# The projection's bank first in attention's PSUM pool, and the last tile's half columns one after the other at the end of a two-layer diffusion backbone

## The chip, the cores and the metric

The kernel runs on one core of a Trainium2 chip. The core has five engines with a queue each: TensorE (PE) for matrix products, VectorE (DVE) and ScalarE (ACT) for elementwise work, GpSimd (POOL), and SyncE (SP), which issues most transfers between the chip's memory (HBM) and the core's SBUF. TensorE writes its products to PSUM, eight banks of 128 rows by 512 float32 values; DVE and ACT read them there. The metric is the device time of one launch in microseconds (us), the median of several runs.

## The reference, cut to what matters

512 latent tokens and 256 context tokens of width 1024 pass through two layers. Layer 0 mixes tokens by windowed attention with 16 query heads and 4 key heads, layer 1 by a gated MLP over chunks of 128 tokens. Each is followed by a dense SwiGLU feed-forward network with hidden width 2816. Both halves of a layer are wrapped in RMS norms and modulated by a conditioning vector:

```python
x = x + g_ml * rmsnorm(y_l, norm_g[i, 1])
f_l = swiglu(modulate(rmsnorm(x, norm_g[i, 2]), sh_fl, sc_fl), ffn_w_in[i], ffn_w_out[i])
x = x + g_fl * rmsnorm(f_l, norm_g[i, 3])
```

The last line, in layer 1, is the end of the program: for each token, the second product of the feed-forward network is divided by the root of its own mean square over all 1024 columns, multiplied by a row of gains, added to `x` and stored.

## The kernel before

Products are made at float32 precision from two rounded parts of each operand ("high", a cast on ACT, and "low", a subtraction on DVE), three matmuls for one: high by high, high by low, low by high. Tokens are handled in four tiles of 128, numbered 0 to 3.

**The order is written out by hand.** Every piece of work is a small function. `at(time, step, ...)` files it in a plan under a name made of the function and its arguments, such as `q_step_2_0` or `c3square_y_0_512`. A long string, `ORDER`, lists all names, and `run_plan` calls the steps in the order of that list. Scheduling is manual: each engine executes its instructions in the order in which the steps issued them, and waits in its queue where an operand or a buffer isn't ready. Times given to `at` matter only for names that the list lacks.

**PSUM pools.** The first stage (norms, transposes, keys, values and the first query projections) uses the pool `psA` with all eight banks, one tile per bank. Its last tiles are two query projections (`q0`, read by `q_rows_0` and `q_rows_1`, L952) and six transposed key tiles (`kT`, `k_turn`, L1030), each read by a cast on ACT into `khi` (L414) and a subtraction on DVE into `klo` (L421). Then `psA` is closed, and attention opens two pools in the same banks: `psL`, with two double-bank tiles for scores (`s_ps`, banks 0-1 and 2-3), and `psR`, on the right side, with four single banks for three tags: `q` (one bank, the projections of later query heads, `q_ps`), `pT` (two banks, transposed probabilities) and `o` (one bank, the product with the values, `o_ps`). A tag gets its banks when it is first asked for, the first tag the lowest, bank 4. One line asks for a tile of `o` ahead of everything, so before the change `o` has bank 4, `q` bank 5, and `pT` banks 6 and 7. A new tile waits for the last reader of the tile of the older pool in its bank, and for no other. In the program as it is laid out, the last tenant of `psA` is `q0` of `q_rows_1` in bank 4, the `kT` of `k_turn_0_0` in bank 5, and the `kT` of `k_turn_2_0` in bank 1.

**Attention.** After the key transposes, TensorE's queue holds `q_step_2_0` to `q_step_2_7` (L872): 24 matmuls that project the third pair of query heads into one `q_ps` tile, from weight unit 3 (`whigh_3_*`, `wlow_3_*`). Behind them stand the first scores `score_0_0` and `score_0_1` (L1110). Then, for 16 blocks of 128 queries by 4 heads: `bound` on DVE (L1116), `exp` on ACT (L1121), `normalise` on POOL (L1137), transposes on TensorE (`turn`, L1143) copied by ACT and DVE (`turned`, L1150), the product with the values into `o_ps` (`value`, L1159), and its copy to SBUF on ACT (`store`, L1165). `store_15` is the last of them. The output projection follows in the pool `psM`, whose tiles take banks 0, 7, 6, 5, 4, 3, 2, 1 in this order: `work_0_0` (L481) writes `y00` to bank 0 and `y01` to bank 7, in turn.

**The end of the program.** In layer 1, the last two units of the feed-forward network's second weight matrix (86 and 87) are multiplied plainly: `plain7_9_t` and `plain7_10_t` (L1868) add their part for token tile `t` to two banks, `y[t][0]` for columns 0 to 511 and `y[t][1]` for 512 to 1023. A whole step is 12 matmuls that alternate between the two banks; tile 3 is done by half columns, `plain7_9_3_(0,)` and so on, 6 matmuls each. Earlier parts of the same sums are added by DVE (`add7_*`, L1858) and must be in the banks before. The operands of units 86 and 87 are `whigh`, `wlow` and `take7_18` to `take7_21`.

For each tile, a chain ends the layer: `square_y` on ACT (L441) gives the sum of squares of each half, `gain_y` on DVE (L1341) multiplies by the gains, then the reciprocal root, then `add_x` on DVE (L1345), then `store` (a transfer that SP issues, L411). ACT and DVE take turns on a bank. For tiles 0, 1 and 2 the root is made by `rstd_y`: a small instruction on DVE (L450) and a power on POOL (L451). For tile 3 it is made on ACT: `bias_y` (DVE, L1328), `root_y` (ACT, L1332), `invert_y` (DVE, L1335), and `add_x` and `store` are issued for each half.

The order of TensorE's steps there, before the change: 9_2, 9_3 columns 1, 9_3 columns 0, 9_0, 10_3 columns 0, 10_3 columns 1, 10_2, 10_0, 9_1, 10_1. So tile 3 is finished early and tile 1 last.

Of the kernel before, what the change touches and what calls it, by code (L numbers as in the profile page):

```python
# [7 lines left out]
F32 = mybir.dt.float32  # L8
# [6 lines left out]
P = 128  # L15
# [372 lines left out]
f1a7_high_4_0 f1a7_low_4_0 f1product7_4_0 f1w7_high_4_2 f1add7_p7_1 f1add7_p7d_1 f1add7_p7d_0 f1w7_low_4_2 f1add7_c12_0  # L388
f1add7_c22_0 f1take7_18 f1a7_high_4_3 f1a7_low_4_3 f1t7_add_3_21 f1take7_19 f1product7_4_1 f1w7_high_4_3 f1product7_4_2
f1w7_low_4_3 f1product7_4_3 whigh_86_1 whigh_87_0 wlow_86_1 f1add7_c21_0 f1add7_c11_0 f1add7_c22_1 whigh_87_1  # L390
f1plain7_9_2 wlow_87_1 f1add7_c21_1 f1plain7_9_3_(1,) wlow_87_0 f1plain7_9_3_(0,) f1plain7_9_0 f1take7_20 f1take7_21
f1plain7_10_3_(0,) c3square_y_0_512 f1plain7_10_3_(1,) c3square_y_512_1024 c3gain_y_0_512 c3bias_y c3root_y
c3gain_y_512_1024 c3invert_y f1plain7_10_2 c3add_x_512_1024 c3store_512_1024 c2gain_y_0_512 c2gain_y_512_1024
f1add7_c12_1 c2square_y_0_512 c2square_y_512_1024 c2rstd_y#4 f1plain7_10_0 c0square_y_512_1024 c0square_y_0_512
c2add_x#4 c0gain_y_0_512 c0gain_y_512_1024 f1plain7_9_1 c0rstd_y#4 c0add_x#4 c0store f1plain7_10_1 c3add_x_0_512
c1square_y_0_512 c1gain_y_0_512 c3store_0_512 c1square_y_512_1024 c1rstd_y#4 c1gain_y_512_1024 c2store c1add_x#4 c1store
""".split()


# [1 line left out]
def backbone_kernel(ctx: ExitStack, tc: tile.TileContext, a, out):  # L401
# [58 lines left out]
    def big(name):  # L460
        return base.tile([P, 2 * D], F32, name=name, tag="big", bufs=2)
# [403 lines left out]
    q_ps = {}  # L865
# [206 lines left out]
    psL_p = psL.__enter__()  # L1072
    psR = pool("psR", space=PSUM, side="right")
    psR_p = psR.__enter__()
    psR_p.tile([P, 512], F32, name="o_ps", tag="o", bufs=1)
    oT = [big("oT0"), big("oT1")]

    def bank_t(name):
# [1180 lines left out]
```

## Time and profile before

| what | us |
|---|---|
| median of three runs | 1101.46 |
| the three runs | 1101.46, 1100.64, 1102.72 |
| the profiled execution, device time | 1101.11 |
| its span, first to last instruction | 1099.3 |

The profile comes from one execution. Its span is 1.81 us shorter than that execution's device time, which itself is 0.35 us below the median. Rows of the timeline have the start in us from the span's start, the duration in us, the engine, the source line, the operation, the tiles written and read, the shapes, how many alike follow each other, and in brackets the engine's idle time before and what ended it. "PEld" is TensorE loading its stationary operand, "SPq" a transfer being issued, not its duration.

### The profile page before, as it was taken

The page shows a single profiled execution, that of the slowest core. Times are in us where ns is not written, and L with a number is a line of the kernel's source. Part 1 is how long each engine was busy: PE and PEld are TensorE (multiplying, and loading weights), DVE is VectorE, ACT ScalarE, POOL GpSimd, SP SyncE. Part 2 cuts the span into 40 slices and gives each one's busy share as a digit, 9 for nine tenths or more (in the row PEclk, how much of TensorE's full clock was granted, in tenths as well). Part 3 has the DMA queues.
Part 4 walks back from the last instruction along what each step waited for, and adds up shares of the span by engine and source line. Part 5 has one row for each costly group of instructions (what it writes and reads, how often), then busy time and mean ns, then how long its engine had stood idle before and what let it go on. Part 6 is the DMA issues. An engine that isn't in the chain of part 4 may idle for free.

```text
span 1099.3 us, 17847 instructions
## 1 busy us (share of the span) xinstructions
PE 1078.4 (98%) x6894; PEld 950.6 (86%) x6894; DVE 941.6 (86%) x1383; ACT 601.9 (55%) x1058; POOL 264.7 (24%) x267
## 2 busy tenths in 40 slices
PE   8979999999999999999999999999999999999997
PEld 5767777778899999998888888888999999998885
DVE  5896998938999999998988878968988798977985
ACT  6455777646654555456655534346544544556562
POOL 1624777435700000002321402007400000003300
PEclk9999999999999999999999999999999999999999
DMA  9764341346225465569964478543243334378831
GB/s 364 259 196 128 107 154 48 115 154 211 87 81 179 154 194 171 197 220 277 229 132 153 137 237 299 179 165 96 77 152 118 135 115 166 94 258 194 209 76 77
DMA packets 50393, 181.26 MB, mean 165 GB/s; under 512 B 5370, under 2 KB 9722, under 8 KB 39172
## 3 DMA queue, kind: packets, MB, share of 16 engines
q1 hardware_dynamic: 42756, 165.44, 43.6%
q0 software_dynamic: 7552, 14.68, 8.0%
q8 instruction: 54, 0.88, 0.3%
q14 instruction: 31, 0.25, 0.1%
HBM read 171.71 MB, written 2.10 MB: 158 GB/s over the span
## 4 chain that ended last, share of the span: by engine, by line
PE 90%; DVE 4%; DMA 1%; POOL 1%; issue 1%; ACT 1%; SPq 0%; DVEq 0%; ACTq 0%; POOLq 0%
PE f L1657 37%; PE y L1841 14%; PE y L481 7%; PE y L1868 6%; PE v L481 4%; PE o_ps L1159 3%; PE s_ps L1110 3%; PE pT_ps L1143 2%; PE q_ps L872 2%; PE fa L475 1%; PE fa L473 1%; PE fa L474 1%; PE u L2079 1%; PE u L2078 1%; PE u L2077 1%; POOL w_lo L421 1%
## 5 line engine op out<-in xcount | busy, mean ns | idle before, releaser
L1657 PE MATMUL f<-H,w_hi 128*128 128x256 f32 x960 | 176.3, 283 | 0.0
L1657 PEld LDWEIGHTS f<-H,w_hi 128*128 128x128 f32 x960 | 149.8, 192 | 0.3
L1657 PE MATMUL f<-H,w_lo 128*128 128x256 f32 x480 | 135.8, 283 | 0.0
L414 ACT CAST w_hi<-w_raw 128x1024 fp32r<-128x1024 f32 x90 | 93.8, 1053 | 50.6 <-PE y L481 15.6
L1841 PE MATMUL y<-w_hi,s 128*128 128x512 f32 x448 | 120.2, 389 | 0.0
L1657 PE MATMUL f<-S,w_hi 128*128 128x256 f32 x640 | 117.5, 283 | 0.0
L421 DVE TENSOR_TENSOR w_lo<-w_raw,w_hi 128x1024 fp32r<-128x1024 f32 (+1 forms) x81 | 96.9, 1200 | 22.6 <-ACT w_hi L414 22.4
L414 ACT CAST w_hi<-T 128x1024 fp32r<-128x1024 f32 x80 | 83.8, 1051 | 54.4 <-PE f L1657 33.4
L421 DVE TENSOR_TENSOR w_lo<-T,w_hi 128x1024 fp32r<-128x1024 f32 x80 | 97.0, 1219 | 11.0 <-ACT w_hi L414 10.6
L1657 PEld LDWEIGHTS f<-S,w_hi 128*128 128x128 f32 x640 | 99.9, 192 | 0.2
L1841 PEld LDWEIGHTS y<-w_hi,s 128*128 128x128 f32 x448 | 84.0, 188 | 17.7 <-ACT r L1849 0.3
L1657 PEld LDWEIGHTS f<-H,w_lo 128*128 128x128 f32 x480 | 92.1, 192 | 0.0
L1657 PE MATMUL f<-S,w_lo 128*128 128x256 f32 x320 | 90.5, 283 | 0.0
L595 POOL DMA_DIRECT2D acc<-acc x8 | 6.9, 866 | 345.4 <-DVE acc L581 339.0
L1664 ACT COPY fc<-f 128x256 f32<-128x256 f32 x120 | 43.1, 373 | 77.0 <-PE f L1657 69.6
L1829 POOL DMA_DIRECT2D t<-in_w x48 | 42.7, 975 | 165.5 <-DMA t<-in_w 87.8
L581 DVE SCALAR_TENSOR_TENSOR acc<-ada_k,sc,acc 128x1024 f32<-128x1024 f32 x56 | 71.6, 1279 | 3.6 <-DMA ada_k<-in_ada 3.3
L1841 PE MATMUL y<-w_lo,s 128*128 128x512 f32 x224 | 69.1, 390 | 0.0
L1657 PE MATMUL f<-H,x 128*128 128x256 f32 x480 | 64.4, 283 | 0.0
L1137 POOL TENSOR_SCALAR p<-p,st 128x512 f32<-128x512 f32 (+1 forms) x64 | 56.0, 907 | 34.0 <-DVE st L1133 26.1
L1116 DVE CUSTOM_DVE_ANT_0 s_ps<-s_ps,mask,nsink 128x512 f32<-128x512 f32 (+1 forms) x64 | 51.3, 820 | 14.8 <-PE s_ps L1110 13.7
L1657 PEld LDWEIGHTS f<-S,w_lo 128*128 128x128 f32 x320 | 61.4, 192 | 0.0
(265 smaller groups left out, 2760.5 us busy)
## 6 DMA issues: line engine op xcount, KB each, us to landing
w_raw<-in_w SPq DMA_DIRECT2D x67, 1024.0 KB, 5.2
ada_k<-in_ada SPq DMA_DIRECT2D x56, 512.0 KB, 4.9
ada_raw<-in_ada SPq DMA_DIRECT2D x12, 1024.0 KB, 6.2
w<-in_w SPq DMA_DIRECT2D x12, 1024.0 KB, 8.2
t<-in_w POOLq DMA_DIRECT2D x48, 256.0 KB, 6.4
ada<-in_ada SPq DMA_DIRECT2D x8, 1024.0 KB, 7.2
t<-in_w SPq DMA_DIRECT2D x8, 1024.0 KB, 8.4
w_raw<-in_w SPq DMA_DIRECT2D x10, 512.0 KB, 9.7
```

What stands on the lines that cost most here:

```text
L414: nc.scalar.copy(out=hi, in_=src)
L421: (eng or nc.vector).tensor_tensor(out=v(lo), in0=v(src), in1=v(hi).bitcast(F32), op=ALU.subtract)
L481: nc.tensor.matmul(dst, l, w[:, n * 512:(n + 1) * 512], start=first and i == 0, stop=last and i == 2)
L581: nc.vector.scalar_tensor_tensor(out=self.acc, in0=self.raws.pop(k), scalar=sc[:, k:k + 1], in1=self.acc, op0=ALU.mult, op1=ALU.add)
L1110: nc.tensor.matmul(dst, q, keys, start=i == 0, stop=i == 1)
L1116: nc.vector.tensor_tensor_reduce(out=s, in0=s, in1=self.msk, scale=-1.0, scalar=nsink[:, h:h + 1], op0=ALU.add, op1=ALU.min, accum_out=sel ...
L1137: nc.gpsimd.tensor_scalar(out=p, in0=p, scalar1=self.st[:, 12 + j:13 + j], scalar2=1.0, op0=ALU.mult, op1=ALU.mult)
L1657: nc.tensor.matmul(dst, l[:, w], r[:, k, :], start=first and k == 0 and j == 0, stop=k == 3 and j == 2, skip_group_check=True)
L1664: nc.scalar.copy(out=self.c[n][:, i * 256:(i + 1) * 256], in_=self.ps[n, 1 if i == 1 else 0])
L1829: nc.gpsimd.dma_start(out=self.tt[:, p * D + 512 * i:p * D + 512 * (i + 1)], in_=a["w"][F2[self.layer] + 1 + 2 * p + i][:, c:c + 512], acc ...
L1841: nc.tensor.matmul(self.bank7(i, j), st[:, c:c + P], w[:, z * 512:(z + 1) * 512], start=i == 1 and p == 0 and l == 0 and z == 0, stop=p == ...
L1868: nc.tensor.matmul(self.y[t][n], st[:, x + t * P:x + (t + 1) * P], parts[h][w][:, n * 512:(n + 1) * 512], start=v == 0 and h == 0 and i == ...
```

## The change

Two edits. The line that asks for a tile of `psR` ahead of everything asks for tag `q` in place of `o`. And the end of `ORDER`, from `plain7_9_2` on, is rewritten.

```diff
@@ ORDER, its last lines @@
-f1plain7_9_2 wlow_87_1 f1add7_c21_1 f1plain7_9_3_(1,) wlow_87_0 f1plain7_9_3_(0,) f1plain7_9_0 f1take7_20 f1take7_21
-f1plain7_10_3_(0,) c3square_y_0_512 f1plain7_10_3_(1,) c3square_y_512_1024 c3gain_y_0_512 c3bias_y c3root_y
-c3gain_y_512_1024 c3invert_y f1plain7_10_2 c3add_x_512_1024 c3store_512_1024 c2gain_y_0_512 c2gain_y_512_1024
-f1add7_c12_1 c2square_y_0_512 c2square_y_512_1024 c2rstd_y#4 f1plain7_10_0 c0square_y_512_1024 c0square_y_0_512
-c2add_x#4 c0gain_y_0_512 c0gain_y_512_1024 f1plain7_9_1 c0rstd_y#4 c0add_x#4 c0store f1plain7_10_1 c3add_x_0_512
-c1square_y_0_512 c1gain_y_0_512 c3store_0_512 c1square_y_512_1024 c1rstd_y#4 c1gain_y_512_1024 c2store c1add_x#4 c1store
+f1plain7_9_2 f1take7_21 f1plain7_9_0 f1add7_c21_1 f1plain7_9_3_(0,) wlow_87_0 f1take7_20 wlow_87_1 f1plain7_10_0
+c0square_y_512_1024 c0square_y_0_512 f1plain7_10_2 c2square_y_0_512 f1plain7_10_3_(0,) c0gain_y_0_512 c0rstd_y#4
+c0gain_y_512_1024 c2square_y_512_1024 f1add7_c12_1 c2gain_y_0_512 c2rstd_y#4 c0add_x#4 c0store c2gain_y_512_1024
+f1plain7_9_1 c3gain_y_0_512 c3square_y_0_512 c3bias_y c2add_x#4 f1plain7_10_1 c1square_y_0_512 c1square_y_512_1024
+c2store c1gain_y_0_512 c1rstd_y#4 c1gain_y_512_1024 c1add_x#4 c1store f1plain7_9_3_(1,) f1plain7_10_3_(1,)
+c3square_y_512_1024 c3root_y c3gain_y_512_1024 c3invert_y c3add_x_0_512 c3store_0_512 c3add_x_512_1024 c3store_512_1024
@@ attention's PSUM pools @@
     psR = pool("psR", space=PSUM, side="right")
     psR_p = psR.__enter__()
-    psR_p.tile([P, 512], F32, name="o_ps", tag="o", bufs=1)
+    psR_p.tile([P, 512], F32, name="q_ps", tag="q", bufs=1)
     oT = [big("oT0"), big("oT1")]
```

After it `q` has bank 4, `pT` banks 5 and 6 (its first tile, of `turn_0_2`, comes before the first of `o`), and `o` bank 7. The order of TensorE's last steps becomes 9_2, 9_0, 9_3 columns 0, 10_0, 10_2, 10_3 columns 0, 9_1, 10_1, 9_3 columns 1, 10_3 columns 1. Tile 0's chain comes first, then tile 2's, tile 1's, and tile 3's second half last; of tile 3's first half, the gains, the squares and the bias are done ahead of tile 1's chain. No instruction is added or removed, and the arithmetic is the same.

More of the change, by code (lines that the diff above doesn't have):

```diff
@@ L390 @@
 f1w7_low_4_3 f1product7_4_3 whigh_86_1 whigh_87_0 wlow_86_1 f1add7_c21_0 f1add7_c11_0 f1add7_c22_1 whigh_87_1
-f1plain7_9_2 wlow_87_1 f1add7_c21_1 f1plain7_9_3_(1,) wlow_87_0 f1plain7_9_3_(0,) f1plain7_9_0 f1take7_20 f1take7_21
-f1plain7_10_3_(0,) c3square_y_0_512 f1plain7_10_3_(1,) c3square_y_512_1024 c3gain_y_0_512 c3bias_y c3root_y
-c3gain_y_512_1024 c3invert_y f1plain7_10_2 c3add_x_512_1024 c3store_512_1024 c2gain_y_0_512 c2gain_y_512_1024
-f1add7_c12_1 c2square_y_0_512 c2square_y_512_1024 c2rstd_y#4 f1plain7_10_0 c0square_y_512_1024 c0square_y_0_512
-c2add_x#4 c0gain_y_0_512 c0gain_y_512_1024 f1plain7_9_1 c0rstd_y#4 c0add_x#4 c0store f1plain7_10_1 c3add_x_0_512
-c1square_y_0_512 c1gain_y_0_512 c3store_0_512 c1square_y_512_1024 c1rstd_y#4 c1gain_y_512_1024 c2store c1add_x#4 c1store
+f1plain7_9_2 f1take7_21 f1plain7_9_0 f1add7_c21_1 f1plain7_9_3_(0,) wlow_87_0 f1take7_20 wlow_87_1 f1plain7_10_0
+c0square_y_512_1024 c0square_y_0_512 f1plain7_10_2 c2square_y_0_512 f1plain7_10_3_(0,) c0gain_y_0_512 c0rstd_y#4
+c0gain_y_512_1024 c2square_y_512_1024 f1add7_c12_1 c2gain_y_0_512 c2rstd_y#4 c0add_x#4 c0store c2gain_y_512_1024
+f1plain7_9_1 c3gain_y_0_512 c3square_y_0_512 c3bias_y c2add_x#4 f1plain7_10_1 c1square_y_0_512 c1square_y_512_1024
+c2store c1gain_y_0_512 c1rstd_y#4 c1gain_y_512_1024 c1add_x#4 c1store f1plain7_9_3_(1,) f1plain7_10_3_(1,)
+c3square_y_512_1024 c3root_y c3gain_y_512_1024 c3invert_y c3add_x_0_512 c3store_0_512 c3add_x_512_1024 c3store_512_1024
 """.split()
```

## The prediction

> **What bounds the kernel now.** I read the page's busy shares first, then what TensorE waited for, then the two places that the change touches, by timeline and by windows.
>
> ```profile
> span 1099.3 us, 17847 instructions
> PE 1078.4 (98%) x6894; PEld 950.6 (86%) x6894; DVE 941.6 (86%) x1383; ACT 601.9 (55%) x1058; POOL 264.7 (24%) x267
> PE q_ps L872 <- DVE klo L421: 7.5, 1, 7.5
> PE s_ps L1110 <- ACT p L1121: 2.0, 3, 1.0
> ```
>
> TensorE is busy for 98% of the span, so time is won only where it idles or after its last matmul. Its waits, the last two lines, show one large one: 7.5 us, once, before a `q_ps` matmul, for a `klo` subtraction. A projection needs no `klo`: it reads `HA` and weights. What it waits for is its bank, which the key tile of `k_turn_0_0` still holds. The timeline of that place:
>
> ```profile
> 73.32 2.78 PE L1030 MATMUL kT<-ident,kr 128*128 128x128 f32 x24
> 73.52 0.60 ACT L952 ACTIVATE q_rot<-q 128x512 f32<-128x512 f32 x1 [1.69 <-PE q L872]
> 74.93 0.68 DVE L421 TENSOR_TENSOR w_lo<-w_raw,w_hi 128x512 fp32r<-128x512 f32 x1
> 77.33 0.68 DVE L421 TENSOR_TENSOR w_lo<-w_raw,w_hi 128x512 fp32r<-128x512 f32 x1
> 82.84 1.28 DVE L421 TENSOR_TENSOR klo<-kT,khi 128x512 fp32r<-128x512 f32 x2
> 83.58 1.22 PE L872 MATMUL q_ps<-HA,w_hi 128*128 128x512 f32 x2 [7.47 <-DVE klo L421]
> 84.15 1.40 DVE L421 TENSOR_TENSOR q_X<-q_rot,q_X 64x512 fp32r<-64x512 f32 x2
> 91.00 0.39 PE L1110 MATMUL s_ps<-khi,q_X 128*128 128x512 f32 x1
> 91.26 0.60 ACT L952 ACTIVATE q_rot<-q_ps 128x512 f32<-128x512 f32 x1 [7.05 <-PE q_ps L872]
> 92.11 0.76 DVE L1116 CUSTOM_DVE_ANT_0 s_ps<-s_ps,mask,nsink 128x512 f32<-128x512 f32 x1 [6.55 <-PE s_ps L1110]
> ```
>
> TensorE ends the transposes at 76.10, idles to 83.58, projects to 91.0, and only then scores. ACT (7.05 us) and DVE (6.55 us) idle for that projection in turn. Windows over the same place (PE busy, granted clock, DMA share, GB/s):
>
> ```profile
> 76.10:83.58 7.48, 0.01 (x2) 0.81 0.72 202
> 83.58:87.51 3.93, 3.93 (x9) 0.50 0.00 0
> 87.51:91.00 3.49, 3.49 (x16) 1.00 0.00 0
> 80.00:81.00 1.00, 0.00 (x0) 0.84 1.00 426
> 82.00:83.00 1.00, 0.00 (x0) 0.50 0.74 139
> 87.00:88.00 1.00, 1.00 (x4) 0.74 0.00 0
> ```
>
> The idle stretch also cost clock: it was half from 80.7 (0.84 in the slice 80 to 81) to 87.5, so that a matmul took 0.43 us (3.93/9) instead of 0.22 (3.49/16). No transfer moves from 83.58 to 91: all of the core waits for the projection.
>
> **Part 1, the bank.** With `q` in bank 4, the first projection waits for the reader of the older tile there, `q_rows_1`: the ACT row at 73.52, done at 74.12. Its other conditions: the weights' low half, row 74.93, done at 75.61; TensorE free at 76.10. So it starts at 76.1. Its fifth step needs the other low half, row 77.33, done at 78.01, and is reached 12 matmuls later, 76.1 + 12 x 0.227 = 78.8 (0.227 is the pitch of the warm matmuls in the last table below). The 24 matmuls end at 76.1 + 5.45 = 81.55, at full clock, since TensorE has worked without a break.
>
> What is late next: the scores. They need the keys of `k_split_0_0`, and the score tile's banks 0-1, which the `kT` of `k_turn_2_0` holds: the second subtraction of the row at 82.84, done at 84.12. The PE row at 83.58 followed its releaser (0.68 after 82.84, so 83.52) by 0.06; so the first score comes at 84.18 and not at 91.00: **6.8 us earlier**. DVE's own chain to 84.12 isn't changed; that TensorE now works beside it costs it nothing, as its 128x512 subtraction took 0.68 us beside the transposes (74.93) and with TensorE idle (77.33). DVE has `q_X` until 85.55 and can then take the first bound, 6.56 us earlier than at 92.11; the 0.26 us of difference is hidden behind the `q_step_3` matmuls that follow the scores on TensorE. `q_rows_2` follows the second pair's casts on ACT, and the next weight unit has landed by 83 (no transfer after). All that comes later was triggered from here, so it moves as one.
>
> Two things are given back. **The clock:** a break from 81.55 to 84.18 remains, 2.6 us. Rows on both sides: the fall at 80.7 came 4.6 us after TensorE stopped (76.10); that at the end came at 1094.44 (0.72 in its slice), 2.6 us after the last matmul (below). A fall thus comes at no fixed distance from the stop, and 2.6 us can be enough.
>
> ```profile
> 1091.24 0.61 PE L1868 MATMUL y<-w_hi,st 128*128 128x512 f32 x2
> 1094.00:1095.00 1.00, 0.00 (x0) 0.00 (x0) 0.91 (x1) 0.00 (x0) 0.02 (x1) 0.72 1.04 414
> ```
>
> Once down, it came back 3.9 us after work resumed (83.58 to 87.51), and those 3.9 us did the work of 2.0. So the price is 0 to 1.9 us. As the gap is just as long as the shorter of the two distances, I take the middle, 0.9: some executions pay, some don't. The Trainium skill, page "TensorE: Matmul & The Clock Gate", section "Why this matters for your kernels", asks for no break above about 3 us and says that a whole idle window brings the half rate back; in Part 1 it gives the free-running window as about 3.4 us. By that rule 2.6 us would cost nothing and the sum would be 0.9 lower; the fall at 1094.44 speaks against it.
>
> **The bank of `o`.** It becomes 7, which `y01` of the output projection takes:
>
> ```profile
> 237.62 0.74 PE L481 MATMUL y<-w_hi,HA 128*128 128x512 f32 x2
> 237.74 0.37 ACT L1165 COPY oT<-o_ps 128x256 f32<-128x256 f32 x1 [0.31 <-PE o_ps L1159]
> ```
>
> The second of these matmuls, at 237.97, must now wait for the ACT copy to 238.11 and 0.06 more: **+0.2 us**. `pT` moves among banks that are long free: nothing.
>
> **Part 2, the end.** The order before, on the timeline:
>
> ```profile
> 1069.94 0.62 PE L1868 MATMUL y<-w_hi,st 128*128 128x512 f32 x2
> 1074.10 1.29 DVE L421 TENSOR_TENSOR st<-act,st 128x512 fp32r<-128x512 f32 x2
> 1079.66 0.60 ACT L441 ACTIVATE junk<-y 128x512 bf16<-128x512 f32 x1 [7.43 <-PE y L1868]
> 1081.08 0.60 ACT L441 ACTIVATE junk<-y 128x512 bf16<-128x512 f32 x1 [0.73 <-PE y L1868]
> 1081.80 0.29 ACT L1332 ACTIVATE ry<-msy,by 128x1 f32<-128x1 f32 x1
> 1081.80 0.69 DVE L1341 TENSOR_TENSOR tmp<-y,row 128x512 f32<-128x512 f32 x1 [0.67 <-ACT junk L441]
> 1082.41 0.15 DVE L1335 RECIPROCAL ry<-ry 128x1 f32<-128x1 f32 x1
> 1082.59 0.75 DVE L1345 SCALAR_TENSOR_TENSOR x<-tmp,ry,x 128x512 f32<-128x512 f32 x1
> 1091.73 0.60 ACT L441 ACTIVATE junk<-y 128x512 bf16<-128x512 f32 x1 [3.80 <-PE y L1868]
> 1093.30 0.68 DVE L1341 TENSOR_TENSOR tmp<-y,row 128x512 f32<-128x512 f32 x1
> 1094.09 1.28 DVE L1345 SCALAR_TENSOR_TENSOR x<-tmp,ry,x 128x1024 f32<-128x1024 f32 x1
> 1096.00:1097.00 1.00, 0.00 (x0) 0.00 (x0) 0.00 (x0) 0.00 (x0) 0.00 (x0) 0.50 0.79 319
> 1097.00:1098.00 1.00, 0.00 (x0) 0.00 (x0) 0.00 (x0) 0.00 (x0) 0.00 (x0) 0.50 0.51 205
> SPq L2255 <- DMA out<-x: 2.2, 1, 2.2
> ```
>
> 96 matmuls run from 1069.94 to about 1091.7: 0.227 each, 2.72 a whole step. Their number stays. Now, the last chain takes 1091.73 to 1095.37 (add's end), because two squares follow each other on ACT, the root goes over DVE and POOL, and the add is 1024 wide. After, the last matmul belongs to the second half of tile 3, one matmul (0.23) after the release at 1091.73, so its square starts at 1091.96. Tile 3's earlier chain gives the rest: square to add 1.51 (1081.08 to 1082.59), the second add some 0.67 behind the first (an estimate: like the two 0.68 us subtractions in 1.29 us at 1074.10, which start 0.6 apart, with a 0.75 us add), 0.75 long: end at 1094.89, 0.48 earlier. DVE must be free of tile 1 by 1092.68, when the second half's gains start (1091.96 + 0.72). Tile 1's last product now ends two half steps, 2.72 us, before the end, so its first square starts at 1091.73 - 2.72 = 1089.01; to its add it needs the same 2.36 us as now (1091.73 to 1094.09), which gives 1091.37, and 1.28 more for the add: 1092.65. It just fits; if not, up to 0.3 us is lost.
>
> The last transfer is half as large. The final 512 KB kept the transfer engines busy for 0.79 + 0.51 = 1.3 us; half saves 0.65. Tile 1's store is issued near 1092.7 and through by 1095; the two halves of tile 3 follow at about 1094.3 and 1094.9, so they don't queue. **Together 1.1 us.** Ends: nothing, if the three last stores crowd, and 1.5.
>
> Can TensorE stall in the new order? `plain7_10_0` comes after 2.5 steps, at 1076.7; the operands (last row 1074.10, done 1075.39) come up to 0.6 later by the new order, 1076.0. `plain7_9_1`, after five, at 1083.5, needs `add7_c12_1`, which now stands on DVE behind tile 0's gains: tile 0's squares start at 1079.7, its gains two squares (1.44) later, and two gains, the small root instruction and `add7_c12_1` take 2.0 more: about 1083.2. Slack 0.3 us: taken as nothing, up to 0.5 lost. Half steps cost about half a whole one: 1.42 from 1079.66 to 1081.08, where two of them stand now.
>
> **Sum.** 1099.3 - 6.8 + 0.9 + 0.2 - 1.1 = 1092.5 us of span. Around the span lie 1.81 us, and the median of the runs is 0.35 above the profiled execution: 1092.5 + 2.16 = **1094.7 us**.
>
> **The rivals.**
> - *The clock never falls in the break of 2.6 us* (the whole-window rule as a mechanism of this kernel): 1093.8. For it: the waits of 1.0 us for `p` left no mark on the clock. Against: the fall at 1094.44. Chance 0.27.
> - *The 6.8 us are lost on the way,* since another engine sets the pace of attention. DVE is the candidate:
>
> ```profile
> 100.00:120.00 20.00, 18.56 (x117) 15.21 (x116) 19.48 (x37) 13.10 (x30) 14.01 (x17) 1.00 0.52 159
> DVE s_ps L1116 <- PE s_ps L1110: 13.7, 11, 6.5
> ```
>   DVE is busy for 19.48 of 20 us there, TensorE for 18.56. But DVE's own start moves by 6.56, and it waited for scores ten more times for 7.2 us. If half is lost: 1098.1. Chance 0.12.
> - *The layout doesn't do what it says,* and the projection still waits for a key tile: only the end pays, 1101.46 - 1.1 = 1100.4, no measurable change. Chance 0.04.
> - *Slower: the clock falls in the break and stays down.* Each 3.9 us at half clock cost 1.9. The rest gains 7.7, so it decides after 7.7 x 2 = 15 us down; 20 us would give 1103.8. Before, one stretch of work was enough to bring it back. Chance 0.02.
>
> **How the numbers follow.** Forecast 0.55, at 1094.7 (1093.8 to 1096); the rivals 0.27, 0.12, 0.04, 0.02. The lower end takes the first rival with the end at its best (0.4) and a median that strays by half the spread of the runs shown: 1092.3. The upper end takes a price of 1.9 for the clock, an end that gains nothing, 0.5 of stall, and part of the half-lost case: 1097.7. This kernel's runs spread by about 0.2%, 2.2 us, which is what can be told from no change: below 1099.3 is faster, 0.93; within, 0.05; slower, 0.02.
>
> **What would show it.** The `q_ps` wait of 7.5 us is gone, and the first `q_ps` matmul stands at 76.1; a break of 2.6 us before the first score, for the `klo` that ends at 84.1; the clock in windows of 84 to 88; `y01` 0.2 us late, for the copy of `o_ps`; `store_15` and the later stages 6 to 7 us earlier; no wait of TensorE before `plain7_9_1`; after the last matmul one square, one root on ACT, two adds. I am wrong if the first score moves but the output projection doesn't, if the first projection still waits for `klo`, or if the last store ends as late after the last matmul as now.

## The result and the profile after

| | us |
|---|---|
| before, median of 4 runs | 1101.05 (1099.93 to 1102.72) |
| changed, median of 4 runs | 1093.41 (1091.35 to 1094.24) |
| ratio | 0.9927, 95% interval 0.9907 to 0.9946 |
| changed, the profiled execution | 1094.24, its span 1092.5 |

The change makes the kernel 0.73% faster, 8.0 us by the ratio, with an interval of 5.9 to 10.2 us. 1094.7 was predicted.

Of the page of the changed kernel, the span and the busy shares; and of its waits, the two that TensorE still has at `s_ps` (total, times, longest):

```profile
span 1092.5 us, 17851 instructions
PE 1078.3 (99%) x6894; PEld 950.4 (87%) x6894; DVE 940.6 (86%) x1383; ACT 602.0 (55%) x1058; POOL 265.9 (24%) x267
PE s_ps L1110 <- DVE klo L421: 2.5, 1, 2.5
PE s_ps L1110 <- ACT p L1121: 1.5, 2, 1.0
```

TensorE does the same work in 6.8 us less. Its wait of 7.5 us before `q_ps` is gone; the wait for `klo` is now the scores', and 2.5 us. The same place on the timeline:

```profile
75.72 0.70 PE L872 MATMUL q_ps<-HA,w_hi 128*128 128x512 f32 x2
81.06 0.39 PE L872 MATMUL q_ps<-HA,w_lo 128*128 128x512 f32 x1
82.59 1.28 DVE L421 TENSOR_TENSOR klo<-kT,khi 128x512 fp32r<-128x512 f32 x2
83.92 0.80 PE L1110 MATMUL s_ps<-khi,q_X 128*128 128x512 f32 x1 [2.47 <-DVE klo L421]
86.03 0.76 DVE L1116 CUSTOM_DVE_ANT_0 s_ps<-s_ps,mask,nsink 128x512 f32<-128x512 f32 x1 [0.73 <-PE s_ps L1110]
```

The projection starts at 75.72, right behind the transposes, and ends at 81.45. The first score comes 7.08 us earlier than before (91.00 to 83.92). But its matmul takes 0.80 us where it took 0.39: the clock is down. Windows that are cut at the clock's own changes (us, PE busy, granted clock, DMA share, GB/s):

```profile
80.46:83.88 3.42, 0.99 (x5) 1.00 0.58 132
83.88:87.29 3.41, 3.37 (x8) 0.50 0.23 55
```

It is half for 3.41 us, and this is where part of the 7.08 us goes: the output projection's first matmul is only 6.11 us earlier (237.62 to 231.51). There the next piece is lost:

```profile
231.51 1.04 PE L481 MATMUL y<-w_hi,HA 128*128 128x512 f32 x2
231.63 0.37 ACT L1165 COPY oT<-o_ps 128x256 f32<-128x256 f32 x1 [0.31 <-PE o_ps L1159]
232.05 0.19 PEld L481 LDWEIGHTS y<-w_hi,HA 128*128 128x128 f32 x1 [0.35 <-ACT oT L1165]
278.67 1.67 PE L1657 MATMUL f<-H,x 128*128 128x256 f32 x12
```

The two matmuls at 231.51 take 1.04 us together, 0.74 before: the second waits for the copy out of `o_ps` that ends at 232.00. From `y` to the first matmul of the feed-forward network it is now 47.16 us (231.51 to 278.67). From there on TensorE has the same distance to its end as before. The end:

```profile
1085.67 0.39 PE L1868 MATMUL y<-w_hi,st 128*128 128x512 f32 x1
1086.16 0.60 ACT L441 ACTIVATE junk<-y 128x512 bf16<-128x512 f32 x1 [1.54 <-PE y L1868]
1086.88 0.29 ACT L1332 ACTIVATE ry<-msy,by 128x1 f32<-128x1 f32 x1
1086.88 0.69 DVE L1341 TENSOR_TENSOR tmp<-y,row 128x512 f32<-128x512 f32 x1
1087.67 1.42 DVE L1345 SCALAR_TENSOR_TENSOR x<-tmp,ry,x 128x512 f32<-128x512 f32 x2
```

One square, one root, two half adds, as laid out. From TensorE's last matmul to the last add's end it takes 3.03 us (1086.06 to 1089.09), where it was 3.51 (1091.86 to 1095.37), and from there to the span's end 3.38 us where it was 3.97.

### The profile page after: what moved, and what is told of

It reads as the page before. It is cut to its first block, busy times and chain, and to the rows that moved or that the text cites. A ratio compares the mean times of both kernels' runs of the same rounds, so it can differ in the third digit from the quotient of the medians.

```text
span 1092.5 us, 17851 instructions
## 1 busy us (share of the span) xinstructions
PE 1078.3 (99%) x6894; PEld 950.4 (87%) x6894; DVE 940.6 (86%) x1383; ACT 602.0 (55%) x1058; POOL 265.9 (24%) x267
## 4 chain that ended last, share of the span: by engine, by line
PE 94%; DVE 3%; ACT 1%; issue 1%; DMA 0%; DVEq 0%; SPq 0%; ACTq 0%
PE f L1657 37%; PE y L1841 13%; PE y L481 7%; PE y L1868 6%; PE v L481 4%; PE s_ps L1110 3%; PE o_ps L1159 3%; PE pT_ps L1143 3%; PE q_ps L872 2%; PE fa L473 1%; PE fa L475 1%; PE fa L474 1%; PE u L2079 1%; PE u L2078 1%; PE u L2077 1%; PE kv L473 1%
## 5 line engine op out<-in xcount | busy, mean ns | idle before, releaser
L1657 PEld LDWEIGHTS f<-H,x 128*128 128x128 f32 x480 | 60.6, 192 | 0.1
```

The source lines that it names most:

```text
L1657: nc.tensor.matmul(dst, l[:, w], r[:, k, :], start=first and k == 0 and j == 0, stop=k == 3 and j == 2, skip_group_check=True)
```

## The experiments

Theory: the bank removed a wait of TensorE, less what the clock and the bank of `o` take back; the end's order is worth 1.0 us by itself. The rivals are that the clock or another engine's pace takes most of it back; that the parts depend on each other; that the tail's gain is all in its last transfer. Ratios below are to the kernel before, timed on the same chip in the same rounds.

| run | median us | ratio, 95% interval |
|---|---|---|
| bank alone | 1094.10 | 0.9943 (0.9931 to 0.9956) |
| tail alone | 1099.68 | 0.9993 (0.9984 to 1.0002) |
| `o` second | 1092.42 | 0.9926 (0.9914 to 0.9939) |
| break filled | 1093.22 | 0.9931 (0.9919 to 0.9944) |
| before, idle filled | 1098.88 | 0.9982 (0.9973 to 0.9991) |
| keys first | 1092.67 | 0.9925 (0.9911 to 0.9939) |
| keys first, low parts early | 1091.38 | 0.9914 (0.9901 to 0.9928) |
| changed, again | 1094.08 | 0.9936 (0.9923 to 0.9950) |
| `o` second, again | 1092.29 | 0.9922 (0.9908 to 0.9935) |
| root on GpSimd, one run | 1093.98 | |
| one store, one run | 1094.06 | |

### The two parts, each alone

The bank without the tail:

```diff
-    psR_p.tile([P, 512], F32, name="o_ps", tag="o", bufs=1)
+    psR_p.tile([P, 512], F32, name="q_ps", tag="q", bufs=1)
```

> The kernel before with the pool's line alone changed (`q` asked for first, the tail's order as before). Theory A (the wait for klo was the whole of the first part, and the two parts add): first q_ps matmul near 75.7, first score near 83.9, the last layer starts about 5.8 us earlier than in the kernel before, the end as before (7.4 us from PE's end to the span's end): about 5.8 to 6.5 us faster than before. Theory B (the first part's gain is mostly won back by the clock and later layers even out what remains): under 4 us, and the tail's order brings the rest. Theory C (the two parts are not independent, because the tail's order only fits a stream that arrives earlier): the sum of this run and of the run with the tail alone misses the whole change by over 1 us.

The tail without the bank is the reverse: that line as before, the end of `ORDER` as changed.

> The changed kernel with `o` asked for first again, so that only the tail's order and its ScalarE root remain. Theory A (1.0 us, as the distance from PE's end to the span's end fell from 7.44 to 6.44): 1.0 us faster than before, the idle PE of 7.5 us ahead of q_ps there again, PE's end where it was. Theory B (the tail is ended by its last store whatever precedes it): 0.6 us, the part that the halved store alone gives. Theory C: nothing, since PE now stalls in the tail: PE's end later by what the end gains.

The timeline of the kernel with the bank alone:

```profile
83.71 0.50 PE L1110 MATMUL s_ps<-khi,q_X 128*128 128x512 f32 x1 [2.47 <-DVE klo L421]
230.18 1.04 PE L481 MATMUL y<-w_hi,HA 128*128 128x512 f32 x2
1086.93 1.29 DVE L1345 SCALAR_TENSOR_TENSOR x<-tmp,ry,x 128x1024 f32<-128x1024 f32 x1
```

and of the one with the tail alone:

```profile
83.01 1.22 PE L872 MATMUL q_ps<-HA,w_hi 128*128 128x512 f32 x2 [6.59 <-DVE klo L421]
1091.17 0.39 PE L1868 MATMUL y<-w_hi,st 128*128 128x512 f32 x1
1093.17 1.42 DVE L1345 SCALAR_TENSOR_TENSOR x<-tmp,ry,x 128x512 f32<-128x512 f32 x2
```

The bank alone gains 6.3 us (4.8 to 7.6), the tail alone 0.8 (a gain of 1.8 to a loss of 0.2). Together that is 7.1, against 8.0 and 7.0 in the two sets of runs of the changed kernel: within these intervals the parts add, which is theory A of the bank alone. The tail's 0.8 us can't be told from nothing by its times; by its profile the end comes 6.42 us after TensorE's last matmul (1091.56), where it was 7.48, and this 1.06 us is its theory A.

One thing was not expected: with the same break of 2.47 us the clock did not fall with the bank alone (the first score takes 0.50 us, against 0.80), and `y` stands at 230.18, 7.44 us earlier than before.

### What the clock costs, and when it falls

Ten matmuls in the break of the changed kernel (`pT` is asked for second there; `...` stands for lines left out):

```diff
+    def keep_busy():
+        ps = psR_p.tile([P, 512], F32, name="o_ps", tag="o", bufs=1)
+        for _ in range(10):
+            nc.tensor.matmul(ps, ws.halves[Q0 + 1, 0][0][:, 0:P], HA[:, 0, :], start=True, stop=True)
...
@@ ORDER @@
-wfetch_4 q_step_2_7 q_rows_2 score_0_0
+wfetch_4 q_step_2_7 keep_busy q_rows_2 score_0_0
```

> The changed kernel with ten matmuls more (their result is read by nobody) between the last q_ps matmul and the first score, which fill the 2.5 us in which PE waits for klo; `pT` is asked for second, so that the banks stay those of the changed kernel. Theory A (the granted clock falls because of that break, and costs 1.7 us where it falls: 3.4 us at half the speed): the fall is gone from the profile; the first score stays within 0.3 us of 83.9, and the bound and all behind it come up to 1.5 us earlier than in the profiled execution of the changed kernel; over all executions 0 to 1.5 us faster than the changed kernel, by how many of its executions fell. Theory B (the fall is not caused by the break): it is still there. Theory C (the fall is gone, yet nothing comes earlier, because DVE with its bounds sets the pace until 100): same time.

And 32 of them in the kernel before, ahead of `q_step_2_0`:

> The kernel before, banks and tail order as they were, with 32 matmuls more (their result is read by nobody) ahead of the first q_ps matmul, in the 7.5 us in which PE stands idle there; they end, at 0.23 us each, just before klo frees bank 5 at 83.5. Theory A (of the 6.3 us that the bank alone brought, some 2 us are the clock's: it fell at 80.7 in the kernel before and was down for 4.3 us in which PE had work): the clock does not fall, q_ps starts within 0.3 us of where it did, and the kernel is 1.9 to 2.2 us faster than before; the other 4 us of the bank's gain are the wait itself. Theory B (the clock's fall costs PE nothing, since DVE sets the pace until 100): the clock does not fall, and the time is that of before within 0.4 us.

The break filled, on the timeline:

```profile
81.05 2.60 PE L1085 MATMUL o_ps<-HA,w_hi 128*128 128x512 f32 x10
83.48 0.46 PE L1118 MATMUL s_ps<-khi,q_X 128*128 128x512 f32 x1
229.89 1.04 PE L481 MATMUL y<-w_hi,HA 128*128 128x512 f32 x2
```

The idle stretch of the kernel before, filled:

```profile
82.83 0.61 PE L872 MATMUL q_ps<-HA,w_hi 128*128 128x512 f32 x2
235.07 0.74 PE L481 MATMUL y<-w_hi,HA 128*128 128x512 f32 x2
```

In neither does the clock fall in this stretch. The price is best read from the first score to `y`, which leaves out when the score came: 146.41 us with the break filled (83.48 to 229.89), 146.47 with the bank alone, 146.53 in the kernel with the root on GpSimd (below), whose clock stayed as well, and 146.62 before. It is 147.59 in the changed kernel's profile (83.92 to 231.51), 147.62 in its second and 147.42 in the kernel with one store, in all of which the clock fell. So the fall costs 0.8 to 1.2 us where it happens. 3.37 busy us at half speed put 1.7 us of work off; some of it comes back, since without the fall TensorE stands waiting once more before 100 (busy 9.57 of the 10 us from 90 to 100 with the break filled, 10.00 in the changed kernel). In the times, filling the break shows nothing that the scatter of about 1 us lets through.

The kernel before paid more. Filled, it is 2.0 us faster (1.0 to 3.0), by theory A; from `q_ps` to `y` it has 152.24 us, where it had 154.04 (`q_ps` itself starts 0.75 us earlier in this execution, where 0.3 was allowed for; this stretch leaves that out, the 2.0 us don't). So of the 6.3 us that the bank gains about 1.8, somewhat under a third, was the clock's, and the rest the wait itself.

When does it fall? The trace records each change of the granted clock. In every run, any two changes lie a whole number of steps of 3.413 us apart (83.88 to 87.29 is one, 87.29 to 1090.81 is 294), and the grid lies elsewhere in each execution. Counted back from a run's last change, the windows of this grid can be laid over TensorE's rows. The kernel with `o` second, once and again, at its end, and the one with one store:

```profile
1082.72:1086.14 3.42, 1.49 (x7) 1.00 0.26 103
```
```profile
1083.06:1086.47 3.41, 1.24 (x6) 1.00 0.26 103
```
```profile
80.64:84.05 3.41, 1.15 (x5) 1.00 0.63 147
1084.15:1087.57 3.42, 1.54 (x7) 1.00 0.25 102
```

Behind the windows with 1.24 and 1.15 us of work the clock fell, at 1086.47 and at 84.05; behind those with 1.49 and 1.54 it stayed. All profiled runs agree, from the first change that the trace records (at 7 to 9 us) on: at full clock, it fell after every window in which TensorE was busy for 1.24 us or less of 3.41 (36%), and after none with 1.49 us or more (44%). The bank alone had 2.50 and 1.86 us in the two windows that shared its break, the changed kernel 0.99 in one. A break of 2.5 us therefore costs something only in the executions in which most of it lies in one window. If the grid lies anywhere with equal chance, and with a bound between 1.92 and 2.17 us of idle time (3.41 less 1.49 and 1.24), this is a share of (3.41 + 2.47 - 2 x 1.92) / 3.41 = 0.60 to 0.45 of all positions, about half. The Trainium skill, page "TensorE: Matmul & The Clock Gate", Part 1, gives a free-running window of 3413 ns, which these distances confirm; its condition for the half rate, at least one idle window, does not hold here, as windows that were a third busy were enough.

The changed kernel was run once more for this:

> The changed kernel itself, for the same rounds. Its clock fell in the break of 2.5 us in one execution that was looked at, and not in the kernel with the bank alone, which has the same break. Theory A (the clock is judged on a grid of 3.413 us that is not tied to the program, and falls at the end of a window in which PE was busy less than some third): it falls in some executions and not in others, which come out about 1.4 us apart; median 1092 to 1094. Theory B (the changed tail order or bank order makes the fall): it falls in all, median 1094.

Median 1094.08 (1093.27 to 1094.51); the clock fell again in the profiled execution (at 84.21, after a window with 0.79 us of work). Of three more kernels with the changed kernel's first part, the one with one store fell too (84.05), the one with the root on GpSimd and the bank alone did not. The median is the one that theory B names, 0.08 us above the range of theory A; it is the kernel with the root on GpSimd, with the same banks and the same order of TensorE's steps, that speaks against B.

The record has the mean granted clock of every execution, and it tells more than the times. A fall of 3.41 us in the break takes it to 0.9984 by itself (1.7 us lost of a span of 1092). The three executions of the changed kernel that were timed beside the profiled one have 0.999: in none of them did the clock fall in the break, and the median of 1093.41, which lies between two of them, holds no price for it. They don't stand apart from the one that paid (1091.35 to 1093.86, against 1094.24). With the bank alone, the two executions at 0.999 took 1093.95 and 1094.10 us, the two at 0.997 1094.94 and 1095.82. That points the way of theory A, but two groups 1.4 us apart are not shown: the scatter is as wide.

### The bank of `o`

```diff
     psR_p.tile([P, 512], F32, name="q_ps", tag="q", bufs=1)
+    psR_p.tile([P, 512], F32, name="o_ps", tag="o", bufs=1)
```

> The changed kernel, which asks for `o` right after `q`, so that o_ps lies in bank 5 and the pT pair in banks 6 and 7. Theory A (the 0.3 us that the shift loses at the first matmul of the next stage, 6.11 to 5.82, is the wait of y's bank 7 for the last copy out of o_ps): the wait vanishes and the kernel is 0.3 us faster than the changed one. Theory B (PE is there too early by whatever is late next): the wait passes to another bank or to the weights, and the time is that of the changed kernel within 0.1 us.

> The changed kernel with `o` asked for second, for the same rounds as the changed kernel. Theory A (the wait of y's bank for the last copy out of o_ps costs 0.29 us): 0.3 us under the changed kernel's median in the same rounds, though the spread of single executions, about 1 us, is larger; from y's first matmul to the next stage's first, 46.86 us instead of 47.16. Theory B: that stretch is 47.16 again and the first run's 46.86 was chance.

Of its timeline, the first run and the second:

```profile
230.02 0.74 PE L481 MATMUL y<-w_hi,HA 128*128 128x512 f32 x2
276.88 1.67 PE L1658 MATMUL f<-H,x 128*128 128x256 f32 x12
```
```profile
230.04 0.74 PE L481 MATMUL y<-w_hi,HA 128*128 128x512 f32 x2
276.91 1.67 PE L1658 MATMUL f<-H,x 128*128 128x256 f32 x12
```

The pair takes 0.74 us again, and the stretch is 46.86 and 46.87 us, as before the change, where the changed kernel has 47.16 and, again, 47.14. The bank of `o` costs 0.29 us, shown twice. In the same rounds the median lies 1.8 us under the changed kernel's, more than that. In both profiled executions the break before the first score was short, 2.06 and 2.18 us, and the clock did not fall; in the five with the changed kernel's or the bare bank's layout it was 2.27 to 2.62. DVE reached this place at slightly different times from run to run (the `q_cos_0` product at 73.55 to 74.76). Whether the layout shortens the break or chance did stays open. It doesn't rule a fall out: another execution of the first set has a mean clock of 0.996, which is less than the fall at the end makes (0.998 in the second profile, where it came 4.25 us before the span's end), and it was the slowest of its set, 1093.61.

### The end, by pieces

The last tile's root as the other tiles have it (in both diffs of this section the names in `ORDER` change with the lines shown):

```diff
-                at(e + .05, c.bias_y)
-                at(e + .12, c.root_y)
-                at(e + .15, c.invert_y)
+                at(e + .15, c.rstd_y)
```

> The changed kernel with the root of its last tile on GpSimd again (small add on VectorE, power on GpSimd, as its other three tiles have it). Theory A (ScalarE's root takes 0.29 us and lies beside the 0.69 us gain; GpSimd's power takes 0.55 us behind a VectorE add of 0.2 us, which nearly fits beside that gain too): the last tile's first add starts 0.1 to 0.2 us later, counted from its square's end, and the end with it. Theory B (the root was a main part of the tail's 1.0 us): 0.4 us or more later.

And one store for the last tile:

```diff
-                    at(e + .6 + .1 * n, c.store, *cs)
+                at(e + .8, c.store, 0, D)
```

> The changed kernel with its last tile stored whole, in one transfer of 512 KB behind its second add, where the changed kernel stores halves of 256 KB behind each add. Theory A (half of the tail's gain is the smaller last transfer): from the last add's end to the span's end 3.9 us as in the kernel before, where the changed kernel has 3.4: 0.5 to 0.65 us later. Theory B (the transfer's fixed part decides): 0.2 us or less.

The ends of the two on DVE's timeline:

```profile
1086.53 0.21 DVE L450 TENSOR_SCALAR ry<-msy 128x1 f32<-128x1 f32 x1
1086.66 0.68 DVE L1341 TENSOR_TENSOR tmp<-y,row 128x512 f32<-128x512 f32 x1
1087.40 1.42 DVE L1345 SCALAR_TENSOR_TENSOR x<-tmp,ry,x 128x512 f32<-128x512 f32 x2
```
```profile
1087.31 1.41 DVE L1345 SCALAR_TENSOR_TENSOR x<-tmp,ry,x 128x512 f32<-128x512 f32 x2
```

With the root on GpSimd, from TensorE's last matmul (1085.71) to the last add's end it is 3.11 us, against 3.03: 0.08. The power lies beside the gains, so the engine of the root hardly matters; what does is that one square and half an add are left behind the last matmul. With one store, 3.55 us pass from the last add (1088.72) to the span's end (1092.27) against 3.38: 0.17 us, and not the 0.5 to 0.65 expected. Windows from the last add's end to the last data of the stores, and from there to the span's end (us, granted clock, DMA share, GB/s), tell why. Before the change, changed, and with one store:

```profile
1095.37:1097.66 2.29, 0.50 0.61 243
1097.66:1099.34 1.68, 0.50 0.00 0
```
```profile
1089.09:1090.79 1.70, 1.00 0.83 308
1090.79:1092.47 1.68, 0.50 0.00 0
```
```profile
1088.72:1091.01 2.29, 0.99 0.57 229
1091.01:1092.27 1.26, 0.50 0.00 0
```

With one store the data is through 0.59 us later than in the changed kernel, 2.29 us after the last add, just as before the change. For the transfer, theory A is right. But the program's end behind the data is 0.42 us shorter, 1.26 us, where all other profiled runs have 1.68 or 1.69. SyncE ends the program with a row of waits for transfers, 0.06 us apart in the trace. In the changed kernel the last store is waited for by the first of the row's last eight, which pass from 1091.16 to 1091.59. With one store less, the last store signals another semaphore, which the last of these eight waits for; the seven ahead of it were passed by then, and it passes at 1091.37. So the 0.59 us that this stretch lost (3.97 to 3.38) is the halved store's, all of it. The first half is on its way when the second is issued, and the data of both passes in one stretch (1089.28 to 1090.79).

### What is late next: the keys

The splits of the first block's keys ahead of the second projection's rope; that projection's add, high and low parts behind the first two bounds and exponents (they are filed in the next stretch of the plan, and `o` is asked for second):

```diff
-q_low_0_1 q_low_0_0 q_swap_1 q_cos_1 k_split_0_1 v_copy_5 q_sin_1 k_split_4_0 q_add_1
-k_split_0_0 k_turn_2_0 k_split_2_0 q_high_1_0 q_low_1_0 q_high_1_1 q_low_1_1 q_step_2_0
+q_low_0_1 q_low_0_0 q_swap_1 v_copy_5 k_split_4_0
+k_split_0_0 k_turn_2_0 k_split_2_0 q_cos_1 k_split_0_1 q_sin_1 q_step_2_0
...
-bound_0_1 exp_0_1 bound_0_0 exp_0_0 whigh_4_1
+bound_0_1 exp_0_1 bound_0_0 exp_0_0 q_add_1 q_high_1_0 q_low_1_0 q_high_1_1 q_low_1_1 whigh_4_1
```

> The changed kernel with `o` asked for second, and with VectorE's and ScalarE's splits of the first block's keys (4_0, 0_0, 2_0) ahead of the second projection's rope; that projection's add and its high and low parts come behind the first two bounds and exponents, into the 2.5 us in which VectorE waits for scores there. Theory A (what is late now is klo, on VectorE, and nothing else): the first score at about 82.2 instead of 83.9, PE's break 0.8 us instead of 2.5, so that the clock cannot fall; the first bound near 83.4 instead of 86.0; y's first matmul up to 1.5 us earlier than in the kernel with `o` second, and the time 0.5 to 1.5 us below it. Theory B (DVE's work up to 100 sets the pace, whatever its order): the first score is earlier, y's first matmul within 0.3 us of that kernel's, time the same.

```profile
82.51 0.50 PE L1115 MATMUL s_ps<-khi,q_X 128*128 128x512 f32 x1 [0.80 <-DVE klo L421]
87.67 0.50 PE L1115 MATMUL s_ps<-khi,q_X 128*128 128x512 f32 x1 [1.23 <-DVE q_X L421]
```

On this kernel's timeline the first score comes 1.0 us earlier than with `o` second alone (83.54), and the third waits 1.23 us for `q_X`: it belongs to the third head of the block, which the second projection serves. `y` stands at 230.12: no gain, though DVE also reached this place 0.7 us later in this execution (`q_cos_0` at 74.41, against 73.69). Neither theory had the new wait; the order made it. It was mended so:

```diff
-whigh_4_0 bound_0_1 exp_0_1 bound_0_0 exp_0_0 q_add_1 q_high_1_0 q_low_1_0 q_high_1_1 q_low_1_1 whigh_4_1 q_step_3_2 q_step_3_3 score_0_2
+whigh_4_0 q_add_1 q_high_1_0 q_high_1_1 bound_0_0 exp_0_0 bound_0_1 exp_0_1 q_low_1_0 q_low_1_1 whigh_4_1 q_step_3_2 q_step_3_3 q_step_3_4 score_0_2
```

> As the kernel with the keys first, but the second projection's add and high parts come ahead of the first two bounds, its low parts right behind them, and one projection step more stands ahead of the third score. Theory A (in the kernel with the keys first the 1.0 us won at the first score was lost at the third, which waited 1.23 us for q_X, the low parts of that second projection): PE's break 0.8 us at the first score, under 0.3 us at the third, the pT turn near 96.5 instead of 97.6, and 0.8 to 1.2 us faster than the kernel with `o` second of the same round. Theory B (DVE's and ScalarE's chain of bounds and exponents up to 100 sets the pace): the breaks are gone there and come back before 100 as waits for p, the pT turn at 97.4 or later, time the same within 0.4 us.

```profile
81.75 0.39 PE L1115 MATMUL s_ps<-khi,q_X 128*128 128x512 f32 x1
95.56 0.60 PE L1148 MATMUL pT_ps<-ident,p 128*128 128x128 f32 x4
228.00 0.74 PE L481 MATMUL y<-w_hi,HA 128*128 128x512 f32 x2
```

No break is left at the first score or the third, and in the window of the grid from 80.61 to 84.03 TensorE is busy throughout. The `pT` turn comes 1.96 us and `y` 2.04 us earlier than in the second run with `o` second (97.52, 230.04), in which DVE reached this place at the same time (`q_cos_0` at 73.54 and 73.55). So DVE's bounds don't set the pace here: theory A. The median is 0.9 us under `o` second's in the same rounds (intervals overlap) and 2.7 us under the changed kernel's, whose fastest run (1093.27) is above this kernel's slowest (1092.91). It is the fastest version that was found.

## Why the prediction was right

- **The bank, 6.8 us.** Right: 7.08 us at the first score, with the conditions as named (transposes end, then `klo`); 0.25 of it lies in DVE's chain, which came that much earlier in this execution.
- **Nothing lost on the way** (rival: half). From the first score to `y`, 146.62 us before and 146.47 with the bank alone: DVE, busy to 97% there, still has slack.
- **The clock, 0 to 1.9 us, taken as 0.9.** That some executions pay and some don't was right, and the measured price is 0.8 to 1.2 us where it falls. The upper end came from the 3.9 us between work's return and the clock's, but what is paid is one window of 3.41 us, less what comes back. The rival in which it never falls was wrong as a rule, though it held in three of the four executions behind the median. Wrong, too, was the reason for the middle: what decides is not the distance from TensorE's stop but how much of one window is idle.
- **The bank of `o`, 0.2 us.** 0.29 by two runs; the wait is the one named.
- **The end, 1.1 us.** 1.06 us in the profiles (7.48 to 6.42, tail alone), and both terms hold: the chain's 0.48 is exact (3.51 to 3.03), by one square and half an add less, and the half-size transfer's 0.65 is 0.59. The two halves do pass in one stretch, where the prediction had them apart. TensorE did not stall before `plain7_9_1`.
- **The sum.** The span was predicted as 1092.5 and is 1092.5 in the profile, of an execution that paid for the clock: 7.08 - 0.97 - 0.29 + 1.06 = 6.88 us, where the prediction had 6.8 - 0.9 - 0.2 + 1.1 = 6.8. That the two agree to a tenth is in part luck, as the errors of the terms cancel. The median, 1093.41, lies 1.3 us under the 1094.7 and nearer to the first rival's 1093.8: three of its four executions paid nothing for the clock, and the 0.35 us that the profiled execution lay below the median before was added, while it lay 0.83 us above it this time.

## What to carry to other kernels

Where a pool takes over the banks of another, the order in which its tags are first asked for decides whose readers each new tile waits for: give the earliest user the bank that is released first, and then check who inherits the last one. Before moving work ahead to fill a wait, list what the instructions behind that wait read: here the third score read what had been put off for the first. Work put behind a program's last matmul is best counted in pieces, since half a chain there is worth its duration, and half a store is worth its data's time when the other half is already on its way. And take an experiment's result apart the same way: the kernel with one store lost 0.59 us in the transfer and won 0.42 behind it.

## What the runs showed of the hardware

The granted clock was set on a grid of 3.413 us that isn't tied to the program: down after windows with TensorE busy for at most 1.24 us of it, kept after those with 1.49 us or more. In the half-clock state, one window with 0.52 us of work (before, 80.69 to 84.10) did not bring it back, one with 3.37 us did. A break of 2.5 us was enough for a fall in some executions, and cost 0.8 to 1.2 us of the 1.7 us that the half clock put off. The end of the program took 1.68 us behind the last store's data, and 1.26 us where the last store came later in SyncE's row of closing waits.
